# A third of gate/up's Strassen products moved out of the main loop, and up's multiplication moved from GpSimd to VectorE

## The chip, the cores and the metric

The kernel runs on one core of one Trainium2 chip. The metric is the device time of one execution in microseconds (us); of several runs the median counts. TensorE (PE) multiplies, VectorE (DVE) and ScalarE (ACT) work on SBUF and on PE's eight result banks, GpSimd (POOL) works on SBUF, and SyncE (SP) issues most DMAs.

## The reference

One decoder block on 2048 tokens of 1024 channels, in float32: a mixer (stick-breaking attention in 8 heads beside a causal pooling) and a dense SwiGLU layer, each between two RMS norms and modulated by a vector c. The change touches the second part alone:

```
h = rmsnorm(x, g_ffn_pre) * (1.0 + scale_f) + shift_f
f = (silu(h @ w_gate) * (h @ w_up)) @ w_down          # 1024 -> 2816 -> 1024
x = x + gate_f * rmsnorm(f, g_ffn_post)
```

## The kernel before

A float32 operand is split into a high and a low part, and a product of two blocks is three matmuls (`mm3`: high by high, low by high, high by low). The first half of the program computes the conditioning vectors, the mixer's projections, the attention and the mixer's output. From about 980 us on it works on gate, up and down. Everything below is about that half.

**Strassen's products.** `h @ w_gate`, `h @ w_up` and the multiplication by `w_down` are each done with seven products of half-size blocks in place of eight. For gate and up the blocks are halves of the 1024 channels (4 blocks of 128 each), the tokens in two halves of 512 within each half (`sb`) of the sequence, and the 2816 columns in 22 blocks of 128, taken as 11 pairs j and j + 11 (`HF` = 11). The weight blocks are a11, a12, a21, a22, with the sums s1 to s4; the token blocks are b11 to b22, with the sums t1 to t4 (L1557, `combine`). The seven products are p1 = a11·b11, p2 = a12·b21, s2·t2, s3·t3, s1·t1, a22·t4 and s4·b22. Each is 4 blocks x 3 = 12 matmuls of 128x512.

**The passes (`inner`, L1311).** p1 and p2 are done ahead of the main loop, in a pass of their own each (`q` = 0 and 1). A pass takes gate's and up's weights and both halves of the sequence as the four blocks of another Strassen scheme: per j seven products of 2 blocks x 3 = 6 matmuls (the banks a, e, f, b, h, i, d), 42 in place of 48. GpSimd makes the weight sums s12 and s34 (L1339 to L1347, four instructions of 256 words per j), ScalarE and VectorE split the operands (`split_by_bank`, L1169: a cast, a copy of it into a bank, a subtraction), VectorE combines the products, and the four results go to HBM (`keep`, L1366, tensor `pd`).

**Token operands.** A pass needs token sums of its own (`inner_sums`, L1196). Those of the second pass are made during the first (`second_operands`), and t1 to t4 for the main loop during the second (`main_operands`, L1618): GpSimd makes t3, t2, t1 and t4 from blocks loaded from `h2d` (the tiles `hs`), t4 is put away in HBM (`lated`) and fetched with b22 at the loop's start (`rest_operands`, L1651; tiles `b_raw` and `t_raw`). Beside that, GpSimd makes the sums of w_down's blocks for later (`down_sums`, L1564, tiles `wd`), one set of four at every 12th step from step 10 on.

**The main loop (`gate_up`, L1518; `matrix`, L1405).** For each half sb and each j it loads p1 and p2 (`px`), and does the five other products of gate and then of up, 12 matmuls each. VectorE takes each product from its bank: u2 = p1 + s2·t2 and so on, and the four results per matrix. Gate's result goes through Silu on ScalarE (L1524). Up's result is written to a tile `cu` in SBUF by VectorE (L1533), and GpSimd multiplies it into gate's (L1534). Then GpSimd makes four sums of the products (L1544) for down. Each half's loop is followed by down (seven products of 11 blocks).

**What sets the order.** The order on PE, ACT, DVE and POOL is that in which the program issues them, step after step (a step is one product, 6 or 12 matmuls); each engine takes its instructions in order and waits on semaphores. The step loop (L2059) issues, at step n: what was put `ahead` for n, the product's matmuls, what was due (`takes`), splits for up to six products ahead (`PAIRS`, L1986), and one piece of the side work (the token operands). SP's order is set by a scheduler. The second pass begins at step 77, the main loop at 154.

## Time and profile before

| | us |
|---|---|
| median of 3 runs | 2237.81 (2234.83 to 2240.35) |
| the profiled execution | 2236.15 |
| its span, first to last instruction | 2234.3 |
| first pass of gate/up, from its first matmul | 983.7 |
| main loop, first half, from | 1204.0 |
| down, first half, from | 1506.3 |
| main loop, second half, from | 1717.0 |
| down, second half, from | 2016.2 |

In the groups of instructions, `xN | busy, mean ns | idle before <-releaser` stands behind a line, an engine, an operation, the tile written and the tiles read: N instructions, their busy time in us, the mean of one in ns, the idle time of the engine ahead of them and what ended it. A row of waits reads: engine, what waited, for whom: us in total, times, longest. A row of stages gives the stretch in us, its length, busy time and number of instructions of PE, PEld (TensorE's weight load), DVE, ACT and POOL, then TensorE's granted clock, the DMA engines' busy share and GB/s. A row of the timeline gives start and duration, both in us.

### The profile page before, as it was taken

To read this page: it belongs to the slowest core of one execution; us is meant where nothing else is said; L and a number is where in the kernel's file an instruction comes from. 1 tells how busy PE (TensorE), PEld (TensorE's weight loads), DVE (VectorE), ACT (ScalarE), POOL (GpSimd) and SP (SyncE) were. 2 spreads that over 40 slices of the span, in tenths; PEclk is the share of its full clock that TensorE was granted. 3 is DMA by queue.
4 is the path that set the end of the run, shared out by engine and by line. 5 is a ranking of instruction groups with operands and counts; after the bars stand their busy time and mean duration, and the time that the engine had idled before them with its cause. 6 is when DMAs were issued, how large, how long until landed. Compare 5 with 4: busy or idle time off the path is not lost.

```text
span 2234.3 us, 34412 instructions
## 1 busy us (share of the span) xinstructions
PE 2201.7 (99%) x10481; PEld 1820.6 (81%) x10481; DVE 1604.3 (72%) x2386; ACT 1353.1 (61%) x2752; POOL 1300.4 (58%) x1702
## 2 busy tenths in 40 slices
PE   8999999999999999999999999999999999999998
PEld 6888888888888888878877888888888888888886
DVE  7874599999999965557767655566877656655566
ACT  6435599898989844457756555545555455544454
POOL 1452277787779955538875777762314887761003
PEclk9999999999999999999999999999999999999999
DMA  9986876534443456678999565558778755648664
GB/s 315 344 284 212 285 205 180 151 105 118 119 122 101 150 169 202 206 235 296 319 326 331 181 197 185 187 193 283 235 221 278 246 188 191 198 148 314 203 192 146
DMA packets 364213, 478.13 MB, mean 214 GB/s; under 512 B 23734, under 2 KB 211706, under 8 KB 361084
## 3 DMA queue, kind: packets, MB, share of 16 engines
q1 hardware_dynamic: 359836, 471.73, 65.8%
q10 hardware_dynamic: 4192, 4.20, 0.7%
q8 instruction: 83, 1.36, 0.3%
q14 instruction: 102, 0.84, 0.1%
HBM read 323.27 MB, written 152.57 MB: 213 GB/s over the span
## 4 chain that ended last, share of the span: by engine, by line
PE 54%; POOL 1%; DVE 1%; DMA 1%; issue 1%; ACT 1%; SPq 0%; DVEq 0%; ACTq 0%; POOLq 0%
PE t_u L69 4%; PE t_u L70 4%; PE t_u L71 4%; PE t_g L70 3%; PE t_g L69 3%; PE t_g L71 3%; PE dn0p L70 3%; PE dn0p L69 3%; PE dn0p L71 3%; PE dn1p L69 3%; PE dn1p L71 3%; PE dn1p L70 3%; PE mix L69 1%; PE mix L70 1%; PE mix L71 1%
## 5 line engine op out<-in xcount | busy, mean ns | idle before, releaser
L952 POOL TENSOR_TENSOR w<-sg,pr 128x512 f32<-128x512 f32 (+2 forms) x320 | 306.3, 957 | 46.4 <-DVE pr L947 14.5
L947 DVE TENSOR_TENSOR_SCAN pr<-pr,carry,begin 128x512 f32<-128x512 f32 x192 | 244.3, 1273 | 0.0
L931 ACT ACTIVATE sg<-z 128x512 f32<-128x512 f32 (+2 forms) x320 | 183.1, 572 | 50.8 <-PE z L929 40.5
L60 DVE TENSOR_TENSOR wtl<-wt,wth 128x512 fp32r<-128x512 f32 (+1 forms) x320 | 190.2, 594 | 19.0 <-ACT wth L59 16.8
L59 ACT CAST wth<-wt 128x512 fp32r<-128x512 f32 (+1 forms) x320 | 181.8, 568 | 11.7 <-PE wt L963 9.3
L933 ACT ACTIVATE pr<-z 128x512 f32<-128x512 f32 (+2 forms) x320 | 182.2, 569 | 0.0
L1534 POOL TENSOR_TENSOR s<-s,cu 128x512 f32<-128x512 f32 x88 | 115.9, 1318 | 111.6 <-DVE cu L1533 102.5
L963 PE MATMUL wt<-ident,w 128*128 128x128 f32 x1088 | 172.3, 273 | 1.5 <-POOL pr L943 1.1
L963 PEld LDWEIGHTS wt<-ident,w 128*128 128x128 f32 x1088 | 134.1, 140 | 32.7 <-POOL pr L943 1.8
L1524 ACT ACTIVATE s<-s 128x512 f32<-128x512 f32 x88 | 55.6, 633 | 163.1 <-DVE s L1523 161.6
L978 PE MATMUL av<-wth,vt 128*128 128x512 f32 (+1 forms) x320 | 126.2, 394 | 0.9 <-ACT o L983 0.8
L70 PE MATMUL dn0p<-w0p_l,g0p_h 128*128 128x512 f32 x308 | 119.9, 389 | 0.9 <-DVE w0p_l L60 0.9
L69 PE MATMUL dn0p<-w0p_h,g0p_h 128*128 128x512 f32 x308 | 119.8, 389 | 0.0
L71 PE MATMUL dn0p<-w0p_h,g0p_l 128*128 128x512 f32 x308 | 119.8, 389 | 0.0
L928 PE MATMUL z<-kt,qt 128*128 128x512 f32 (+2 forms) x320 | 118.6, 371 | 0.7 <-ACT pr L933 0.6
L979 PE MATMUL av<-wtl,vt 128*128 128x512 f32 (+1 forms) x320 | 117.7, 368 | 1.3 <-DVE wtl L60 1.2
L929 PE MATMUL z<-kt,qt 128*128 128x512 f32 (+2 forms) x320 | 116.9, 365 | 0.0
L69 PE MATMUL dn1p<-w1p_h,g1p_h 128*128 128x512 f32 x292 | 113.6, 389 | 0.0
L70 PE MATMUL dn1p<-w1p_l,g1p_h 128*128 128x512 f32 x292 | 113.6, 389 | 0.0
L71 PE MATMUL dn1p<-w1p_h,g1p_l 128*128 128x512 f32 x292 | 113.6, 389 | 0.0
L944 DVE TENSOR_TENSOR_SCAN pr<-pr,zero,begin 128x128 f32<-128x128 f32 (+3 forms) x128 | 111.5, 873 | 1.7 <-ACT pr L933 1.7
L1181 DVE TENSOR_TENSOR u_s_l<-u_s,rounded 128x512 fp32r<-128x512 f32 x63 | 43.3, 688 | 90.8 <-ACT rounded L1180 90.8
(774 smaller groups left out, 7172.5 us busy)
## 6 DMA issues: line engine op xcount, KB each, us to landing
pd<-p_c SPq DMA_DIRECT2D x88, 256.0 KB, 4.6
px<-pd SPq DMA_DIRECT2D x22, 1024.0 KB, 6.5
g<-in_w_gate_dram SPq DMA_DIRECT2D x42, 512.0 KB, 4.2
u<-in_w_up_dram SPq DMA_DIRECT2D x42, 512.0 KB, 5.3
wc<-in_w_cond_dram SPq DMA_DIRECT2D x32, 512.0 KB, 7.5
qt<-qd SPq DMA_DIRECT2D x64, 256.0 KB, 4.0
kt<-kd SPq DMA_DIRECT2D x96, 128.0 KB, 3.3
vt<-vd SPq DMA_DIRECT2D x48, 256.0 KB, 3.8
```

The lines of the kernel that those rows point to most:

```text
L59: nc.scalar.copy(hi, src)
L60: low.tensor_tensor(lo, src, raw(hi), ALU.subtract)
L69: nc.tensor.matmul(ps, lh, rh, start=first and i == 0, stop=False)
L70: nc.tensor.matmul(ps, lh, rl, start=False, stop=False)
L71: nc.tensor.matmul(ps, ll, rh, start=False, stop=last and i == n - 1)
L928: nc.tensor.matmul(z[:, 0:L], qt[:, 0, i * P:(i + 1) * P], keys, start=True, stop=False)
L931: nc.scalar.activation(sg[:, 0:L], z[:, 0:L], AF.Sigmoid, scale=0.125)
L933: nc.scalar.activation(pr[:, 0:L], z[:, 0:L], AF.Sigmoid, scale=-0.125)
L947: nc.vector.tensor_tensor_scan(keys, keys, begin, carry, ALU.mult, ALU.bypass)
L952: nc.gpsimd.tensor_tensor(w[:, 0:L], sg[:, 0:L], pr[:, 1:L + 1], ALU.mult)
L963: nc.tensor.transpose(wt[:, i * P:(i + 1) * P], wss[u][i][:, b * P:(b + 1) * P], ident)
L978: nc.tensor.matmul(av[:, lo0:], vb, wh[:, lo0:], start=first, stop=False)
```

## The change

A third product, a22·t4, leaves the main loop for a third pass (`NQ` = 3), so that the steps before the main loop are 231 and the loop has four products per matrix and j. The third pass's token operands (t4 of both halves of the sequence and their inner sums) are made on GpSimd during the second pass (`third_operands`), the main loop's t1 to t3 during the third (now three sums per block in place of four), and t4 no longer goes through HBM. The sets of sums for down stand at the steps of `DOWN_AT`: five in the first pass, three in the second and three in the third (before: six begin in the first pass and five in the second). In `inner_sums` the first difference goes from VectorE to GpSimd, but not for the first pass's operands.

In the main loop p1 and the third product are copied by ScalarE into a result bank (`to_bank`), so that VectorE's add reads the bank; up's add now writes its result back into the bank and VectorE multiplies it into gate's tile, in place of `cu` and GpSimd. px has six blocks in place of four (one load in the second half of the sequence, two in the first). Banks are given out anew: the main loop has five banks for products and three for the copies.

```
+NQ = 3
+DOWN_AT = (10, 22, 34, 46, 58, 82, 106, 130, 156, 176, 196)
-    pd = [dt(f"pd{sb}", [P, NF // 2, 4, TB]) for sb in range(2)]
+    pd = [dt(f"pd{sb}", [P, NF // 2, 2 * NQ, TB]) for sb in range(2)]
-    MAIN = ("t2", "t3", "t1", "t4", "b22")
+    MAIN = ("t2", "t3", "t1", "b22")
...
-        nc.vector.tensor_tensor(x11, x12, x11, ALU.subtract)
+        (nc.vector if by is split else nc.gpsimd).tensor_tensor(x11, x12, x11, ALU.subtract)
...
-                (nc.scalar if m in (2, 5) else nc.sync).dma_start(st[n].rearrange("p (k n) -> p k n", k=HK), rows_of(src, q * HK, j))
+                (nc.scalar if m in (4, 5) else nc.sync).dma_start(st[n].rearrange("p (k n) -> p k n", k=HK), rows_of(src, min(q, 1) * HK, j + q // 2 * HF))
...
+        banked = {}
+        def to_bank(q):
+            if low_ps is not None:
+                banked[q] = low_ps(f"p{q}{name}")
+                nc.scalar.copy(banked[q], first(q))
...
         def take_p6(ps):
-            st["u2"] = plus("u2", ps, next(first_two()))
+            st["u2"] = plus("u2", ps, first(0))
+            take(0, 0, banked.get(0), first(1), first(0))
         def take_p7(ps):
             st["u3"] = plus("u3", ps, st["u2"])
+            take(1, 0, banked.get(2), st["u3"], first(2))
...
-             step("a22", "t4", lambda ps: take(1, 0, ps, st["u3"]), 4 if turn_back else 1),
              step("s4", "b22", lambda ps: take(0, 1, ps, st["u4"]))]
...
             s = ss[i, tb]
-            u = ft("cu", f"cu{sb}_{j}_{i}{tb}")
-            nc.vector.tensor_tensor(u, ps, rest, ALU.add)
-            nc.gpsimd.tensor_tensor(s, s, u, ALU.mult)
+            if ps is None:
+                u = ft("cu", f"cu{sb}_{j}_{i}{tb}")
+                nc.vector.tensor_tensor(u, other, rest, ALU.add)
+                nc.gpsimd.tensor_tensor(s, s, u, ALU.mult)
+            else:
+                nc.vector.tensor_tensor(ps, ps, rest, ALU.add)
+                nc.vector.tensor_tensor(s, s, ps, ALU.mult)
...
+    def third_operands():
+        ys["p3"] = inner_tiles("p3", opools["0"], "ya", "v14", "v32", "y22")
...
+        for u in range(2 * HK):
+            t = 6 + 8 * u
+            for n, k in zip((3, 1, 0, 2), (6, 5, 4, 4)):
+                at(t - k if u else 0, lambda u=u, n=n: load(u, n))
+            for k, args in enumerate(((1, 3, 1, ALU.subtract), (0, 1, 0, ALU.add), (2, 2, 0, ALU.subtract))):
+                at(t + k, lambda u=u, args=args: add(u, *args))
+            if u % 2:
+                for k in range(8):
+                    at(t + 3 + k, lambda i=u // 2: more(i))
...
-    g_ps = banks(4, 2, 3, 0, 1, 5)
-    d_ps = banks(6, 7, 3, 0, 1, 5, 4, 2), banks(4, 2, 1, 5, 6, 7, 3, 0)
+    g_ps = banks(2, 3, 5, 4, 0)
+    d_ps = banks(6, 7, 1, 4, 0, 5, 3, 2), banks(0, 5, 3, 2, 6, 7, 1, 4)
```

What stands on GpSimd in the second pass, around the second block of tokens. `hs` are the token tiles and sums, `wd` the sums for down, `p_4` the weight sums of j = 4. Before:

```order
L1342 TENSOR_TENSOR p_4_s_14783<-p_4_s_14783,p_4_320_14683 128x256
L1561 TENSOR_TENSOR hs_1_1_14617<-hs_1_3_14677,hs_1_1_14617 128x512
L1346 TENSOR_TENSOR p_4_s_14798<-p_4_320_14683 128x256
L1347 TENSOR_TENSOR p_4_s_14798<-p_4_320_14683,p_4_s_14783 128x256
L1561 TENSOR_TENSOR hs_1_0_14649<-hs_1_1_14617,hs_1_0_14649 128x512
L1561 TENSOR_TENSOR wd_512_14751<-wd_512_14755,wd_512_14751 128x512
L1561 TENSOR_TENSOR hs_1_3_14677<-hs_1_3_14677,hs_1_0_14649 128x512
L1561 TENSOR_TENSOR wd_0_14749<-wd_512_14751,wd_0_14749 128x512
L1561 TENSOR_TENSOR wd_512_14755<-wd_512_14755,wd_0_14749 128x512
L1561 TENSOR_TENSOR hs_1_2_14721<-hs_1_2_14721,hs_1_0_14649 128x512
```

Now, where L1642 are the token sums and L1205 to L1209 the inner sums:

```order
L1205 TENSOR_TENSOR hs_0_2_14443<-hs_0_2_14604,hs_0_2_14443 128x256
L1206 TENSOR_TENSOR hs_0_2_14604<-hs_0_2_14604 128x256
L1342 TENSOR_TENSOR p_4_s_14763<-p_4_321_14652 128x256
L1343 TENSOR_TENSOR p_4_s_14763<-p_4_s_14763,p_4_321_14652 128x256
L1208 TENSOR_TENSOR hs_0_2_14604<-hs_0_2_14604,hs_0_2_14443 128x256
L1209 TENSOR_TENSOR hs_0_2_14443<-hs_0_2_14443,hs_0_2_14604 128x256
L1347 TENSOR_TENSOR p_4_s_14779<-p_4_321_14652 128x256
L1348 TENSOR_TENSOR p_4_s_14779<-p_4_321_14652,p_4_s_14763 128x256
L1642 TENSOR_TENSOR hs_1_1_14725<-hs_1_3_14710,hs_1_1_14725 128x512
L1642 TENSOR_TENSOR hs_1_0_14748<-hs_1_1_14725,hs_1_0_14748 128x512
L1642 TENSOR_TENSOR hs_1_2_14750<-hs_1_2_14750,hs_1_0_14748 128x512
```

Three token sums take the place of four for a unit, there are eight units in place of four, and the inner sums have come in between; of the sums for down a set stands in this stretch before, and none now.

What stands on VectorE while up's products of j = 8 are taken, in the first half of the sequence. `t_u` and `b_u` are products in their banks, `u2u` to `u4u` partial sums, `s` gate's results, `g_9_s_l` low parts of the next weights. Before:

```order
L1454 TENSOR_TENSOR u2u_8_18088<-t_u_8_18051,px_8_17705 128x512
L1533 TENSOR_TENSOR cu_8_00_18090<-px_8_17705 128x512
L1181 TENSOR_TENSOR g_9_s_l<-g_9_s_17998,rounded 128x512
L1454 TENSOR_TENSOR u3u_8_18114<-t_u_8_18075,u2u_8_18088 128x512
L1181 TENSOR_TENSOR g_9_s_l<-g_9_321_17887,rounded 128x512
L1533 TENSOR_TENSOR cu_8_11_18138<-t_u_8_18101,u3u_8_18114 128x512
L1454 TENSOR_TENSOR u4u_8_18141<-t_u_8_18101,u2u_8_18088 128x512
```

Now, where `p0u` and `p2u` are the copies in the bank:

```order
L1450 TENSOR_TENSOR u2u_8_19094<-t_u_8_19055,px_8_18698 128x512
L1547 TENSOR_TENSOR p0u_8_19051<-p0u_8_19051,px_8_18698 128x512
L1548 TENSOR_TENSOR s_8_00_18983<-s_8_00_18983,p0u_8_19051 128x512
L1182 TENSOR_TENSOR g_9_s_l<-g_9_321_18900,rounded 128x512
L1450 TENSOR_TENSOR u3u_8_19121<-t_u_8_19081,u2u_8_19094 128x512
L1547 TENSOR_TENSOR p2u_8_19077<-p2u_8_19077,u3u_8_19121 128x512
L1548 TENSOR_TENSOR s_8_10_19015<-s_8_10_19015,p2u_8_19077 128x512
L1182 TENSOR_TENSOR g_9_s_l<-g_9_s_19053,rounded 128x512
L1450 TENSOR_TENSOR u4u_8_19148<-t_u_8_19108,u2u_8_19094 128x512
```

Behind each of up's adds stands the product that GpSimd had, and it reads what the add has just written.

What stands on SP ahead of the main loop. `b_raw` and, in the change, the tiles `hs_*_3` are b22; `t_raw` is t4. Before:

```order
L1516 DMA px_0_15625<-pd_164 128x2048
L1367 DMA pd_165<-p_9_c_15685 128x512
L1659 DMA b_raw<-h2d_124 128x512
L1659 DMA b_raw<-h2d_125 128x512
L1659 DMA b_raw<-h2d_126 128x512
L1659 DMA b_raw<-h2d_127 128x512
L1659 DMA t_raw<-late_158 128x512
L1659 DMA t_raw<-late_159 128x512
```

Now (b22's other three blocks stand further up):

```order
L1627 DMA hs_2_3_17025<-h2d_126 128x512
L1368 DMA pd_161<-p_7_c_16753 128x512
L1368 DMA pd_160<-p_8_c_16797 128x512
L1368 DMA pd_161<-p_8_c_16811 128x512
L1368 DMA pd_160<-p_8_c_16826 128x512
L1420 DMA u_0_321_16850<-in_w_up_dram 128x8x128
L1368 DMA pd_161<-p_8_c_16860 128x512
L1420 DMA g_1_320_17002<-in_w_gate_dram 128x8x128
L1368 DMA pd_160<-p_9_c_16900 128x512
L1368 DMA pd_161<-p_9_c_16915 128x512
L1368 DMA pd_160<-p_9_c_16927 128x512
L1520 DMA px_0_16902<-pd_160 128x2048
```

b22's loads have moved ahead of px, and t4's are gone.

More of the change, by code (lines that the diff above doesn't have):

```diff
@@ L1378, in take_p5 @@
         def take_p5():
[L1379 removed]
+            st["u4"] = t = ft("gf" if not q and m and m % 2 == 0 else "u4", f"u4{name}")
             if not q:
@@ L1554, in gate_up @@
         g[0].ahead.insert(0, (8, lambda: first_products_load(sb, j)))
+        if not sb:
+            g[0].ahead.insert(1, (8 if j else 2, lambda: third_products_load(j)))
         return g[:3] + u[:3] + g[3:] + u[3:] if sb == at == 0 else g + u
@@ L1635, in main_operands @@
             done, coming = [], list(order) if i + 1 < HK else []
-            for at, (n, t) in enumerate(itertools.chain(combine(nc.gpsimd, *(raw[i, k] for k in range(4))), [(None, None)] * 2)):
+            sums = itertools.islice(combine(nc.gpsimd, raw[i, 0], raw[i, 1], None, raw[i, 3]), 3)
+            for at, (n, t) in enumerate(itertools.chain(sums, [(None, None)] * 2)):
                 if done:
                     put(*done.pop(), split_by_bank)
-                if n == "t4":
-                    later(2, lambda i=i, t=t: nc.sync.dma_start(lated[i], t))
-                elif n:
+                if n:
                     done.append((ops[n], cols, t))
@@ L1951, in back, with main @@
             nonlocal g_ps, low_ps
-            g_ps, low_ps = (banks(1, 5, 4, 2, 6), None) if first else (banks(7, 3, 0, 1, 5, 6), banks(4, 2))
+            g_ps, low_ps = (banks(0, 5, 3), None) if first else (banks(2, 6, 7, 1, 4), banks(0, 5, 3))
+        def main():
+            nonlocal low_ps
+            low_ps = banks(6, 7, 1)
         r, at, left = [], {}, []
-        for q in range(2):
-            at[second_operands if q == 0 else main_operands] = len(r)
+        for q in range(NQ):
+            at[(second_operands, third_operands, main_operands)[q]] = len(r)
             for j in range(HF):
@@ L1961, in halves @@
         at[rest_operands] = len(r) - 2
-        for i in range(HF):
+        for i, k in enumerate(DOWN_AT):
             for n, op in zip((0, 6, 7, 8, 9), down_sums(i)):
-                r[10 + 12 * i + n].ahead.append((0, op))
+                r[k + n].ahead.append((0, op))
         for sb in range(2):
@@ L1967, in halves @@
                 s = gate_up(sb, (n - 1) % HF if sb else n, n)
+                if not sb and not n:
+                    s[0].ahead.insert(0, (0, main))
                 if sb and n < 2:
-                    s[0].ahead.append((0 if n == 0 else 5, lambda n=n: back(n == 0)))
+                    s[0].ahead.insert(0, (0 if n == 0 else 5, lambda n=n: back(n == 0)))
                 r += s[:1] + left + s[1:]
```

120 lines of the change are left out of this document (61 added, 59 removed).

## The prediction

> **What bounds the kernel now.** The page's first part, busy time by engine, and then the stages of the second half with each engine's busy time, the granted clock, the DMA share and GB/s:
>
> ```profile
> PE 2201.7 (99%) x10481; PEld 1820.6 (81%) x10481; DVE 1604.3 (72%) x2386; ACT 1353.1 (61%) x2752; POOL 1300.4 (58%) x1702
> ```
> ```profile
> 1003.00:1102.00 99.00, 99.00 (x439) 81.99 (x438) 75.72 (x126) 72.11 (x138) 81.33 (x87) 1.00 0.90 301
> 1102.00:1204.00 102.00, 98.34 (x432) 80.36 (x430) 77.35 (x127) 62.75 (x117) 80.52 (x80) 1.00 0.98 329
> 1260.00:1500.00 240.00, 240.00 (x1061) 198.72 (x1060) 138.32 (x211) 122.47 (x210) 181.10 (x140) 1.00 0.59 190
> ```
> TensorE (PE) is busy in all of the first pass of gate/up (1003 to 1102) and of the main loop (1260 to 1500), at the full clock of 1.00. Only the second pass (1102 to 1204) loses time, 3.7 of 102 us, and there the DMA engines are at 0.98. A busy PE is no proof that it works at its peak, so I read the spacing of its instructions in the timeline: the first matmuls of two neighbouring products of the main loop, 12 matmuls apart, and of two products of the second pass, 6 apart.
>
> ```profile
> 1218.02 0.39 PE L69 MATMUL t_u<-t3h,u_s_h 128*128 128x512 f32 x1
> ...
> 1220.74 0.39 PE L69 MATMUL t_u<-t1h,u_s_h 128*128 128x512 f32 x1
> ```
> ```profile
> 1145.04 0.39 PE L69 MATMUL ep<-v14p2h,p_s_h 128*128 128x512 f32 x1
> ...
> 1146.40 0.39 PE L69 MATMUL fp<-v32p2h,p_s_h 128*128 128x512 f32 x1
> ```
> 2.72 / 12 and 1.36 / 6 are both 0.2267 us. So a matmul costs 0.2267 us of the span in either place; its duration of 0.39 us overlaps its neighbours'. The Trainium skill, "TensorE: Matmul & The Clock Gate", section Back-to-back issue gap, gives 131 ns sustained for 512 columns; by it the sum below would be 66 x 0.131 = 8.6 us. The trace does not agree; its 0.2267 is used.
>
> PE's waits, whole span, the rows that lie behind 980 us:
>
> ```profile
> PE f_pt L134 <- DVE p_s_l L1181: 2.5, 1, 2.5
> PE ap L69 <- DVE u2p L1385: 2.1, 1, 2.1
> PE t_u L69 <- DVE p_c L1371: 1.4, 1, 1.4
> PE ip L69 <- ACT p1p L1376: 1.0, 1, 1.0
> PE dn0p L70 <- DVE w0p_l L60: 0.9, 1, 0.9
> PE ep L69 <- ACT p1p L1376: 0.9, 1, 0.9
> PE ep L69 <- DVE p_c L1371: 0.7, 1, 0.7
> ```
> Two (2.5 and 1.0) lie at the entry to the first pass, which the change leaves nearly alone. Three (2.1, 0.9, 0.7) are the second pass's 3.7 us, 1.4 is the entry to the main loop, 0.9 lies in down's first half. What ends last in the second pass stands in the chain of waits of that stretch:
>
> ```profile
> 1170.02 1.25 POOL hs L1561
> 1171.27 1.24 POOL wd L1561
> 1172.50 1.24 POOL hs L1561
> 1173.77 0.63 ACT t2h L1173
> ```
> GpSimd (POOL) is late with the token sums (hs), ScalarE (ACT) waits for one of them, and what is queued behind it on ACT reaches PE late.
>
> **What leaves and comes on PE.** The third product (a22 by t4) leaves the main loop: 11 pairs of columns x 2 matrices x 2 halves of the tokens x 12 matmuls = 528, at 0.2267 us 119.7 us. It comes back as a third pass of 11 x 7 products x 6 = 462 matmuls, 104.7 us. Net 66 matmuls, **-15.0 us**. No reason excludes that this whole term counts, as PE is what ends last nearly everywhere; it is lost only where another engine becomes late. So each cover is worked out, stage by stage.
>
> **The third pass's own engines.** It does per pair of columns (42 matmuls, 9.52 us) what the second does now. In the second pass's row above DVE is busy 77 and ACT 63 of 102 us, with the preparation of token operands included. The third pass has less to prepare (12 sums of 512 words on POOL in place of 16). Both hide behind PE. Cost 0; without that cover it would be what goes over 9.52 us per pair.
>
> **POOL in the second pass.** This is the tight place. The groups of POOL in it, and POOL's waits there:
>
> ```profile
> L1561 POOL TENSOR_TENSOR wd<-wd,wd 128x512 f32<-128x512 f32 x20 | 25.9, 1296 | 10.7 <-DMA wd<-in_w_down_dram 7.4 <-DMA hs<-h2d 2.4 <-DMA pd<-p_c 0.6
> L1561 POOL TENSOR_TENSOR hs<-hs,hs 128x512 f32<-128x512 f32 x16 | 20.7, 1295 | 4.1 <-DMA hs<-h2d 4.0
> L1341 POOL TENSOR_TENSOR p_s<-p 128x256 f32<-128x256 f32 x9 | 6.7, 742 | 0.6 <-DMA p<-in_w_up_dram 0.6
> ```
> Afterwards the pass holds 24 token sums (8 units of 3) and 12 sums for down (three sets of four, at steps 82, 106 and 130; the row's 20 are five sets), each 1.30 us: 46.8 us. At 0.74 us each it holds 16 inner sums and 44 weight sums: 44.4 us. Together 91 of 104.7 us, where now it is 80.5 of 102 and over 10 more of waiting for DMAs. Between the first token sum (step 83) and the last inner sum (step 145) stand 36 long and 50 short ones in the order, 46.8 + 37.0 = 83.8 us, against 62 steps x 1.36 = 84.3 us of PE. That is 99%: POOL keeps up only if it hardly waits. Two things give it room. The last operand is written at step 148 and read at 156, 8 steps or 10.9 us later; and half as many sets for down leave fewer loads to wait for. The pass's DMAs move tiles of 256 KB, as the stored products do:
>
> ```profile
> pd<-p_c SPq DMA_DIRECT2D x88, 256.0 KB, 4.6
> ```
> 44 products stored are 11.5 MB, 22 loads of weights 5.8, down's sums 6.3 (12 read, 12 written), 32 loads of tokens 8.4, together 32.0 MB in 104.7 us or 306 GB/s, under the row's 329. I take the stalls of this pass at what they are now, 3.7 us, a change of **0**. From below, all 3.7 go. From above, POOL's waits stay at 14.8 us (10.7 + 4.1) on top of 83.8: 98.6 - 84.3 = 14.3 us late, of which nothing is covered: +14.3 - 3.7 = +10.6 us.
>
> **Moving the multiplication.** Of the 88 multiplications of up none stays on POOL. In a pair of columns (96 matmuls, 21.8 us, now 27.2) DVE has 8 low parts, 6 sums, 8 adds and 4 products: 26. The nearest rows for the new product (one operand in the bank, one in SBUF, result in SBUF) are the low part against `rounded`, then the add that it follows; the POOL row is what goes:
>
> ```profile
> L1181 DVE TENSOR_TENSOR u_s_l<-u_s,rounded 128x512 fp32r<-128x512 f32 x27 | 18.6, 689 | 38.9 <-ACT rounded L1180 38.9
> ...
> L1533 DVE TENSOR_TENSOR cu<-t_u,u3u 128x512 f32<-128x512 f32 x16 | 11.1, 692 | 13.4 <-PE t_u L71 12.5 <-POOL u_s L1439 0.9
> ```
> ```profile
> L1534 POOL TENSOR_TENSOR s<-s,cu 128x512 f32<-128x512 f32 x36 | 46.9, 1302 | 49.6 <-DVE cu L1533 49.6
> ```
> 26 x 0.69 = 17.9 of 21.8 us, 82%, where the main loop's row says 138 of 240 (58%). The up half alone has 15 of them in 10.9 us. Starts of DVE in the timeline, two independent instructions and then one that reads what the one before wrote:
>
> ```profile
> 1306.61 0.69 DVE L1454 TENSOR_TENSOR u2u<-t_u,px 128x512 f32<-128x512 f32 x1
> 1307.21 0.69 DVE L1533 TENSOR_TENSOR cu<-px 128x512 f32<-128x512 f32 x1
> 1307.81 0.68 DVE L1181 TENSOR_TENSOR g_s_l<-g_s,rounded 128x512 fp32r<-128x512 f32 x1
> ```
> ```profile
> 1065.75 0.69 DVE L1393 TENSOR_TENSOR u3p<-hp,u2p 128x512 f32<-128x512 f32 x1
> 1066.47 0.69 DVE L1371 TENSOR_TENSOR p_c<-ep,u3p 128x512 f32<-128x512 f32 x1
> ```
> Spacing 0.60, and 0.72 behind a dependence. The up half: 15 x 0.60 + some 8 x 0.12 = 10.0 of 10.9 us; gate's 11 take under 8. If it runs over, five product banks and operands split six products ahead hold PE for some 4 products (10.9 us) until gate's half catches up. The Trainium skill, "VectorE: DVE Perf Modes", section The DRAIN you can't avoid, lets no next operation start before the pipe is empty, which speaks against loading DVE more: 15 x 0.69 = 10.4 of 10.9 us. The 0.60 spacing does not bear that out. Cost **0**; bounds 0 and the end of the third rival below.
>
> POOL keeps eight sums of weights and four of the products, by the page's row
>
> ```profile
> L1544 POOL TENSOR_TENSOR gs<-s,s 128x512 f32<-128x512 f32 x44 | 60.8, 1381 | 3.4
> ```
> 8 x 1.30 + 4 x 1.38 = 15.9 of 21.8 us. That gains nothing, since PE doesn't wait for it in this loop.
>
> The new copies into the bank, 86, go to ACT; its rows in the main loop, and the nearest one to the copy (a full bank, in the second pass):
>
> ```profile
> L1524 ACT ACTIVATE s<-s 128x512 f32<-128x512 f32 x36 | 22.8, 632 | 68.4 <-DVE s L1523 67.0 <-DMA ga0s<-gs 1.4
> L1180 ACT COPY rounded<-u_s_h 128x512 f32<-128x512 f32 x36 | 21.3, 591 | 1.1
> ...
> L1173 ACT CAST u_s_h<-u_s 128x512 fp32r<-128x512 f32 x27 | 16.5, 610 | 14.8 <-PE b_u L70 10.3 <-POOL u_s L1446 4.5
> ```
> ```profile
> L1376 ACT COPY p1p<-ap 128x512 f32<-128x512 f32 x10 | 5.9, 587 | 21.0 <-PE ap L71 21.0
> ```
> Per pair 8 splits at 0.61 + 0.59 (cast, then the copy `rounded`), 4 Silu at 0.63 and 4 copies at 0.59: 14.5 of 21.8 us. A copy waits for its px load, and behind it on ACT are the splits for products six steps on; a late px would cost PE only beyond some 4 products. Cost 0.
>
> **Entry to the main loop.** Now the first px load, four of b22 and four of t4 go out nearly together; afterwards b22's stand ahead of px on the SP queue and t4's are gone, but px comes in two loads, each waiting for a tile of a pass that is ending. The nearest price is the 1.4 us wait there now. I keep it: **0**, from -1.4 to +1.4. The main loop's extra load is half as much px again, 0.5 MB per 21.8 us, 24 GB/s on a row of 190: 0.
>
> **Down and its ends.** Same work on other banks, 12 token sums for 16 in its first half; the 0.9 us may go. 0, from -0.9 to +0.9.
>
> **Sum.** The profiled execution took 2236.15 us (span 2234.3), 1.7 under the median of 2237.81, within the three runs' 2234.83 to 2240.35. 2236.15 - 15.0 = 2221.2; by the median **2222.8 us**.
>
> **Rivals.**
> *The waits go as well.* Fewer loads in the second pass and b22 ahead of px take away 3.7 + 1.4 + 0.9 = 6.0 us: 2216.8. For it: every one of these waits follows a DMA or POOL. Against: POOL has more to do there. 0.16.
> *POOL becomes the bound of the second pass.* Worked out above, from +3 to +10.6 us: 2226 to 2233.4. For it: 99%. Against: a POOL that lags finds its loads landed, and so waits less. 0.24.
> *Slower: the token loads close a circle.* A unit's last token tile takes the slot of the unit before, so it loads only once the third sum there has read it, and the next two sums wait for it: landing + 2 x 1.30 us per unit, against 8 steps or 10.9 us. SP is in order, so product stores, and through their tiles DVE, queue behind the waiting load. The landing of the token loads in the second pass:
>
> ```profile
> DMA to landing us min/median/max: 3.3/4.7/6.5
> ```
> Free up to 8.3 us. The gain is used up, and 6.7 us more, when 8 x (landing - 8.3) reaches 21.7, from a landing of 11.0 us. At 12 us: 29.6 - 15.0 = +14.6, or 2252.4. Against: 6.5 at most now, under a higher load. 0.07, with DVE in the main loop: were its 26 operations to take 0.85 us each (22.1 us), it would lose 0.3 x 22 pairs = 7 us, no more.
>
> **How the numbers follow.** Forecast 0.53, rivals 0.16, 0.24 and 0.07. About 0.3% (6.7 us, to 2231.1) is what a measurement of this kernel can tell. Faster: 0.53 + 0.16 and 0.08 of POOL's = 0.77; same: its other 0.16; slower 0.07. The range takes the lower rival and POOL's upper end: 2217 to 2234.
>
> **What would show it.** Right: 66 matmuls fewer at 0.2267; PE whole in the third pass and both main loops; PE's waits behind 980 us about 9.5 us. Wrong: waits on POOL's sums or on ACT behind them around steps 83 to 156 (POOL as the bound); SP waiting for the token sums with landings over 8 us (the circle); PE waiting in the main loop for a bank that DVE holds.

## The result, and the profile after

The changed kernel takes **2316.27 us** (median of 4 runs, 2314.20 to 2318.91), the kernel before 2238.85 (4 runs, 2234.83 to 2240.35). The ratio is 1.0349, with a 95% interval of 1.0331 to 1.0367: slower by 77 us, where 15 us less were forecast. The forecast of 2222.8 is missed by 93.5 us. (The title's "third" is to be read as one product, the third to leave the loop after p1 and p2: five products per matrix become four.)

The stages of the second half, from the starts of their first matmuls in the timelines. "Forecast" is the kernel before with the prediction's terms (104.7 us for the pass, 264 matmuls at 0.2267 us less per main loop, the rest unchanged):

| us | before | forecast | after |
|---|---|---|---|
| passes of gate/up | 220.2 | 324.9 | 320.5 |
| main loop, first half | 302.4 | 242.5 | 274.8 |
| down, first half | 210.7 | 210.7 | 215.2 |
| main loop, second half | 299.2 | 239.4 | 299.4 |
| down, second half, to the end | 218.1 | 218.1 | 220.7 |

The passes came out 4.4 us better than forecast. All of the loss lies in the two main loops (32.3 and 60.0 us) and in the steps of down behind them. The page's busy time by engine, and the windows of the second pass, the third pass and the two main loops (length, busy time of PE, PEld, DVE, ACT, POOL, granted clock, DMA share, GB/s):

```profile
PE 2228.1 (96%) x10415; PEld 1816.3 (78%) x10415; DVE 1690.6 (73%) x2555; ACT 1412.2 (61%) x2879; POOL 1242.9 (54%) x1694
```
```profile
1096.00:1200.00 104.00, 104.00 (x461) 86.11 (x460) 82.71 (x137) 68.61 (x131) 90.53 (x100) 1.00 0.95 317
1200.00:1305.00 105.00, 105.00 (x465) 86.95 (x464) 82.63 (x135) 67.01 (x125) 65.81 (x67) 1.00 0.84 281
1330.00:1570.00 240.00, 224.22 (x938) 173.19 (x937) 159.53 (x250) 131.49 (x232) 141.43 (x111) 1.00 0.70 221
1820.00:2080.00 260.00, 227.00 (x916) 176.78 (x915) 163.03 (x254) 131.17 (x229) 148.91 (x118) 0.95 0.63 208
```
In both passes PE works without a gap. In the main loops it does not, and no other engine is near its limit there: DVE, the busiest, is at 66% and 63%. The second loop has a lower granted clock as well. PE's waits behind 980 us, the eight largest:

```profile
PE t_g L71 <- DVE s L1533: 23.1, 17, 3.5
PE b_g L71 <- DVE s L1548: 14.7, 17, 1.4
PE b_u L71 <- DVE s L1533: 6.0, 18, 1.4
PE t_g L71 <- DVE u3u L1450: 4.2, 11, 0.4
PE dn1p L71 <- DVE s L1548: 3.6, 2, 2.5
PE b_g L71 <- ACT b22h L1174: 3.2, 1, 3.2
PE f_pt L135 <- DVE p_s_l L1182: 2.4, 1, 2.4
PE dn0p L71 <- DVE s L1548: 2.4, 2, 1.2
```
PE waits for banks that DVE has not emptied: by gate's sum (s, L1533) or by up's multiplication (s, L1548). Yet DVE is idle a third of the time. What it waits for shows where gate's half of a pair runs. ACT in one such half, from one Silu (L1534) to the last, then DVE in the same stretch:

```profile
1443.96 0.63 ACT L1534 ACTIVATE s<-s 128x512 f32<-128x512 f32 x1 [2.54 <-DVE s L1533]
1444.50 0.60 ACT L1174 CAST u_s_h<-u 128x512 fp32r<-128x512 f32 x1
1445.13 0.59 ACT L1181 COPY rounded<-u_s_h 128x512 f32<-128x512 f32 x1
1447.86 0.63 ACT L1534 ACTIVATE s<-s 128x512 f32<-128x512 f32 x1 [2.14 <-DVE s L1533]
...
1451.65 0.63 ACT L1534 ACTIVATE s<-s 128x512 f32<-128x512 f32 x1 [2.02 <-DVE s L1533]
...
1454.84 0.63 ACT L1534 ACTIVATE s<-s 128x512 f32<-128x512 f32 x1 [0.91 <-DVE s L1533]
```
```profile
1429.03 0.68 DVE L1533 TENSOR_TENSOR s<-b_g,u4g 128x512 f32<-128x512 f32 x1
...
1443.25 0.68 DVE L1533 TENSOR_TENSOR s<-p0g,px 128x512 f32<-128x512 f32 x1
1445.81 0.69 DVE L1182 TENSOR_TENSOR u_s_l<-u,rounded 128x512 fp32r<-128x512 f32 x1 [1.89 <-POOL s L1558]
1446.42 0.68 DVE L1450 TENSOR_TENSOR u3g<-t_g,u2g 128x512 f32<-128x512 f32 x1
1447.13 0.69 DVE L1533 TENSOR_TENSOR s<-p2g,u3g 128x512 f32<-128x512 f32 x1
1449.73 0.69 DVE L1182 TENSOR_TENSOR u_s_l<-u_s,rounded 128x512 fp32r<-128x512 f32 x1 [1.90 <-ACT rounded L1181]
...
1450.93 0.68 DVE L1533 TENSOR_TENSOR s<-t_g,u3g 128x512 f32<-128x512 f32 x1
...
1454.12 0.68 DVE L1533 TENSOR_TENSOR s<-b_g,u4g 128x512 f32<-128x512 f32 x1
```
Read the two together: Silu (1443.96), cast, `rounded` on ACT; at its end (1445.72) DVE's low part (1445.81), u3, s; at its end (1447.82) the next Silu (1447.86). Six operations, each standing behind the one before, on two engines that take their queues in order: a **closed circle** of 3.90 us for a product that takes PE 2.72. (The releaser POOL in the third DVE row was done at 1444.88; `rounded` ends there.) DVE's four sums of gate stand at 1443.25, 1447.13, 1450.93 and 1454.12: 10.87 us for three products, 8.16 on PE. From the last sum of one pair (1429.03) to the first of the next (1443.25) it is 14.22 us for five products, 13.60 on PE: up's half, in which DVE is nearly full, can't make it good. So DVE's cycle is 10.87 + 14.22 = 25.09 us a pair, and PE, through its five banks, is held to it:

```profile
1429.86 0.47 PE L71 MATMUL t_g<-t2h,g_s_h 128*128 128x512 f32 x1 [0.18 <-DVE s L1533]
...
1440.35 0.47 PE L71 MATMUL b_g<-b22h,g_s_h 128*128 128x512 f32 x1 [1.01 <-DVE s L1548]
...
1454.95 0.47 PE L71 MATMUL t_g<-t2h,g_s_h 128*128 128x512 f32 x1 [0.19 <-DVE s L1533]
```
1454.95 - 1429.86 = 25.09 us, and 8 x 2.72 would be 21.76. (Each wait costs PE some 0.25 us more than its row says: at the 1.01 us of 1440.35 two matmuls start 1.40 and 0.31 us behind the ones before them, 1.26 over twice 0.2267.)

In the second loop something is added. 21.6 of t_g's 23.1 us behind gate's sum lie there, and ACT's waits in that loop (1795 to 2095 us) have a row that the first loop's have not:

```profile
ACT g_s_h L1174 <- POOL g_s L1442: 18.9, 8, 3.2
```
GpSimd's sum of gate's next weights comes late, and ScalarE's split waits for it inside the circle. In the run "circle closed" at the end of the experiments (SyncE's order pinned and a slot of its own at the turn, the circle as it is) this wait is gone, and the second loop takes 281.9 us in place of 299.4; which of the two edits did it is not shown.

The circle was there before. ACT in the kernel before, two Silus of neighbouring products:

```profile
1325.03 0.63 ACT L1524 ACTIVATE s<-s 128x512 f32<-128x512 f32 x1 [1.77 <-DVE s L1523]
...
1328.15 0.63 ACT L1524 ACTIVATE s<-s 128x512 f32<-128x512 f32 x1 [1.35 <-DVE s L1523]
```
3.12 us there too, more than PE's 2.72. But one in five products (s3·t3) had no Silu, the sum s11 stood ahead of u4, and DVE had room in up's half.

### The profile page after: what moved, and what is told of

The parts are those of the page before. It is cut to its first block, busy times and chain, and to the rows that moved or that the text cites. A ratio compares the mean times of both kernels' runs of the same rounds, so it can differ in the third digit from the quotient of the medians.

```text
span 2315.3 us, 34805 instructions
## 1 busy us (share of the span) xinstructions
PE 2228.1 (96%) x10415; PEld 1816.3 (78%) x10415; DVE 1690.6 (73%) x2555; ACT 1412.2 (61%) x2879; POOL 1242.9 (54%) x1694
## 5 line engine op out<-in xcount | busy, mean ns | idle before, releaser
L1534 ACT ACTIVATE s<-s 128x512 f32<-128x512 f32 x88 | 55.6, 632 | 163.1 <-DVE s L1533 160.6
L1182 DVE TENSOR_TENSOR g_s_l<-g_s,rounded 128x512 fp32r<-128x512 f32 x63 | 43.2, 685 | 95.0 <-ACT rounded L1181 93.1
L1558 POOL TENSOR_TENSOR gs<-s,s 128x512 f32<-128x512 f32 x44 | 58.4, 1326 | 100.4 <-DVE s L1548 78.0
```

## The experiments

**Theories.** 1: the circle. 2: the three banks that splits and copies share are held by the multiplications. 3: VectorE has too much to do with the multiplication itself. All edits are against the changed kernel unless said otherwise.

| run | median us | ratio to before, 95% interval |
|---|---|---|
| late Silu | 2239.39 | 1.0009, 1.0000 to 1.0018 |
| s11 ahead of u4 | 2310.63 | 1.0331, 1.0315 to 1.0346 |
| multiplication on GpSimd | 2270.03 | 1.0147, 1.0132 to 1.0162 |
| no copies into banks | 2309.34 | 1.0323, 1.0306 to 1.0340 |
| three passes, old operations | 2284.72 | 1.0217, 1.0203 to 1.0231 |
| low part late | 2253.83 | 1.0077, 1.0063 to 1.0090 |
| late Silu, own slot | 2233.36 | 0.9983, 0.9974 to 0.9992 |
| before, multiplication on VectorE | 2236.81 | 0.9997, 0.9988 to 1.0006 |
| late Silu, own slot, two on GpSimd | 2253.33 | 1.0071, 1.0058 to 1.0084 |
| late Silu, own slot, all on GpSimd | 2263.06 | 1.0116, 1.0100 to 1.0131 |
| longer Silu | 2355.36 | 1.0527, 1.0513 to 1.0542 |
| longer Silu, late, own slot | 2247.49 | 1.0045, 1.0031 to 1.0059 |
| no multiplication | 2242.41 | 1.0024, 1.0014 to 1.0033 |
| late Silu, own slot, no multiplication | 2302.85 | 1.0287, 1.0269 to 1.0304 |
| pinned SyncE: circle closed | 2304.34 | 1.0303, 1.0285 to 1.0322 |
| pinned SyncE: circle open | 2250.54 | 1.0069, 1.0051 to 1.0087 |
| pinned SyncE: open, no multiplication | 2229.96 | 0.9970, 0.9960 to 0.9980 |
| pinned SyncE: open, all on GpSimd | 2261.43 | 1.0115, 1.0099 to 1.0131 |

**Late Silu.**

```
-            nc.scalar.activation(s, s, AF.Silu)
+            later(1, lambda: nc.scalar.activation(s, s, AF.Silu))
```


> The changed kernel with each Silu of the main loop issued one product later on ScalarE, so that it no longer stands between VectorE's sum and the next split. Theory 1 (a closed circle of in-order queues in gate's half: Silu, cast, rounded on ScalarE, then low part, u and sum on VectorE, then the next Silu; some 3.8 us per product where TensorE needs 2.72): the circle is open, most of the 80 us goes, 2225 to 2245 us, and TensorE's waits in the main loops fall from about 60 to under 20 us. Theory 2 (the three banks shared by the splits and the copies are held by the multiplications) and theory 3 (VectorE is overloaded by the multiplication itself): neither banks nor VectorE's work change, 2305 to 2318 us.

2239.39 us: 77 us less, as theory 1 had it. The first main loop falls from 274.8 to 244.3 us. The longest wait that stays stands at the turn into the second loop (257.0 us). PE, ACT and POOL of this run there:

```profile
1814.98 0.77 PE L71 MATMUL t_g<-t2h,g_s_h 128*128 128x512 f32 x1 [8.32 <-DVE s L1533]
```
```profile
1812.21 0.62 ACT L1174 CAST g_s_h<-g_s 128x512 fp32r<-128x512 f32 x1 [11.05 <-POOL g_s L1442]
```
```profile
1807.26 1.26 POOL L1558 TENSOR_TENSOR gs<-s,gs 128x512 f32<-128x512 f32 x1 [8.16 <-DMA ga1s<-gs]
```
POOL's fourth sum waits for a store to free its slot, the weight sums stand behind it on POOL, the split behind them on ACT, the product behind that.

**s11 ahead of u4.** The two lines of `take_p5` change places. In up's half u4 then reads the bank after the sum was written back, so s01 has another value; the operations are the same.

> The changed kernel with the old order in take_p5: the sum s11 ahead of u4 on VectorE. Theory 1: one VectorE operation of 0.6 to 0.7 us leaves the circle in one of four products of gate, 22 times: 13 to 15 us less, 2300 to 2304 us. Theories 2 and 3: the same operations and banks, within 4 us of 2316.

2310.63 us, 5.6 us less, under half of what one operation in 22 circles should give. The sign fits theory 1, the size doesn't, and why was not settled.

**Multiplication on GpSimd.**

```
-                nc.vector.tensor_tensor(ps, ps, rest, ALU.add)
-                nc.vector.tensor_tensor(s, s, ps, ALU.mult)
+                here = sb and j == HF - 1
+                u = ps if here else ft("cu", f"cu{sb}_{j}_{i}{tb}")
+                nc.vector.tensor_tensor(u, ps, rest, ALU.add)
+                (nc.vector if here else nc.gpsimd).tensor_tensor(s, s, u, ALU.mult)
```


> The changed kernel with up's multiplication back on GpSimd through an SBUF tile in 21 of the 22 pairs of columns (the pair at which the halves turn keeps it on VectorE); copies into the banks and the order of u4 stay. Theory 3: VectorE has 4 operations fewer per pair, the loss goes, 2225 to 2250 us. Theory 1: gate's half is as before, only up's share of the waits (b_u 6.0, a part of b_g's 14.7 us) can go, 2285 to 2318 us. Theory 2: the banks are free one operation (0.6 us) sooner in up's half, 2290 to 2310 us.

2270.03 us, 46 us less: between the ranges, and in none of the three. Theory 1 alone is too small, theory 3 alone too large. VectorE's share in up's half counts, as what could have made good the circle's delay.

**No copies into banks.**

```
-            if low_ps is not None:
+            if turn_back and low_ps is not None:
...
-                nc.gpsimd.tensor_tensor(s, s, u, ALU.mult)
+                nc.vector.tensor_tensor(s, s, u, ALU.mult)
```


> The changed kernel without the copies of stored products into banks in 21 of the 22 pairs: both products are read from SBUF, and the sum for up goes to an SBUF tile and is multiplied there, on VectorE as well. The three banks then serve the splits alone, and ScalarE has 4 operations fewer per pair. Theory 2: no split waits for a bank that a multiplication holds (43 us of ScalarE's waits in the two loops), most of the loss goes, 2235 to 2260 us. Theory 1: the circle keeps its six operations and loses at most the copies that stand in ScalarE's queue in gate's half, 2 x 0.59 us per pair, 26 us: 2290 to 2316 us. Theory 3: VectorE's work is the same, 2305 to 2318 us.

2309.34 us, 7 us less; theory 2's 2235 to 2260 is far off. It is no clean test, since operations of VectorE that now read SBUF alone got longer: the sum cu<-px took 1.39 us on the mean in 218 us of the first loop (the next run shows how).

**Three passes, old operations.** The last three edits together, with `take(1, 1, ...)` ahead of u4; at the one pair that keeps the write into the bank, up's u4 again reads the sum.

> The changed kernel with its three passes and four products, but with the operations around them as they were: multiplication on GpSimd through SBUF, stored products read from SBUF without copies, s11 ahead of u4 (at the pair where the halves turn up keeps VectorE and its copies). Theory 1, the circle alone: gate's half still has four products in a row that each go through Silu, split, u and sum, so loss remains; from the run with the multiplication on GpSimd (2270.0) the two other edits take 6 + 7 us by their own runs: 2250 to 2262 us. Theory 3 (the new work on VectorE and ScalarE is the loss): all of it goes, and the prediction's sum holds, 2218 to 2234 us. GpSimd stands at 21.1 of 21.8 us per pair, which can add to either.

2284.72 us, over both ranges. The new operations are not what made the change slow: with the old ones it is slow as well, and 15 us slower than with the copies kept and the multiplication on GpSimd. What the trace has to set against those 15 us are DVE's rows: first two groups in 218 us of the first loop (from SBUF alone, and with one operand in a bank), then two operations and, last, POOL's two beside the second of them:

```profile
L1533 DVE TENSOR_TENSOR s<-px 128x512 f32<-128x512 f32 x9 | 16.0, 1782 | 0.0
...
L1450 DVE TENSOR_TENSOR u3g<-t_g,u2g 128x512 f32<-128x512 f32 x9 | 6.1, 682 | 0.0
```
```profile
1403.44 0.68 DVE L1544 TENSOR_TENSOR cu<-px 128x512 f32<-128x512 f32 x1
...
1410.99 1.79 DVE L1533 TENSOR_TENSOR s<-px 128x512 f32<-128x512 f32 x1
```
```profile
1410.94 1.28 POOL L1446 TENSOR_TENSOR u_s<-u,u_s 128x512 f32<-128x512 f32 x1
1412.19 1.74 POOL L1550 TENSOR_TENSOR s<-s,cu 128x512 f32<-128x512 f32 x1
```
A sum of two SBUF operands takes DVE 0.68 us in a gap of POOL and 1.79 beside it, inside the circle; with an operand in a bank it is 0.68 on the mean, with POOL busy 192 of the 218 us. The changed kernel's copies into banks avoid that: its sums of p0g and p2g take 0.68 and 0.69. That these longer sums make up the 15 us is argued, not shown: no run takes them away alone.

**Low part late.**

```
+        low = lambda: nc.vector.tensor_tensor(lo, src, both, ALU.subtract)
+        later(2, low) if late else low()
```
(`late` for gate's operands in the main loop; it comes behind the next product's u and sum.)

> The changed kernel with Silu where it was, but with VectorE's low part of gate's operands issued behind the next product's u and sum instead of ahead of them. It opens the circle on the other engine, with the same instructions on ScalarE in the same order. Theory 1: the same gain as with the late Silu, 2235 to 2255 us. Rival: what helped there was Silu's place in ScalarE's queue by itself (splits that are no longer late for TensorE): no gain, 2305 to 2320 us.

2253.83 us, 62 us less, with Silu where it was. The circle opened on the other engine gives most of it as well, with ScalarE's instructions and their order unchanged.

**Late Silu, own slot.**

```
-            s3, s2, s4 = (ft("gs", f"g{n}{sb}_{j}") for n in ("s3", "s2", "s4"))
+            s3, s2, s4 = (ft("p1" if sb and at == 0 and n == "s4" else "gs", f"g{n}{sb}_{j}") for n in ("s3", "s2", "s4"))
```


> Late Silu, and at the turn of the halves the last of GpSimd's four sums (s4) goes to an SBUF slot of its own (p1, idle there) instead of a gs slot that waits for a store. In the run with the late Silu alone GpSimd waited 8.2 us there, ScalarE 11.1 us behind it and TensorE 8.3 us behind that, at 1806 to 1815 us, with a granted clock of 0.84 in that stretch. If the slot is the cause: 9 to 13 us less than 2239.4, 2226 to 2231 us. If the loads of weights behind it in SyncE's queue are late anyway: 2234 to 2240 us.

2233.36 us, 6 us less where 9 to 13 were expected of the slot: the 8.3 us wait is gone, but the second loop still takes 252.2 us. This version beats both kernels, the one before by 0.17% only: less than the prediction's 0.3%, though the interval of these 11 runs leaves out 1.

**Before, with the multiplication on VectorE.** One word in the kernel before, `nc.gpsimd` to `nc.vector` at L1534.

> The kernel before with up's multiplication on VectorE (both operands in SBUF), nothing else changed: four operations more per pair of columns in a loop of five products per matrix, 27.2 us. Theory 1: five products leave VectorE and the circle slack, within 5 us of before. Theory 3: VectorE's multiplication delays what is queued behind it whatever the loop, at least a third of the 46 us that its return to GpSimd gave: slower by 15 us or more.

2236.81 us, no change, although the operation took longer than the 0.69 us that it takes with an operand in a bank (a stretch of the first loop):

```profile
L1534 DVE TENSOR_TENSOR s<-s,cu 128x512 f32<-128x512 f32 x37 | 33.8, 914 | 1.3
```
In a loop of five products VectorE has room for it.

**Two, or all, on GpSimd with the circle open.** The edit of the third run, for `tb` = 1 alone (and gate's s11 ahead of u4), or for all.

> Late Silu and the own slot at the turn, and two of up's four multiplications (s11 and s01) back on GpSimd through SBUF, with s11 ahead of u4 in gate's half only. In the run it is built on, TensorE still waited 7.4 us in 14 places for a bank that an up multiplication on VectorE holds (b_g behind L1548), and lost about half a microsecond per pair. If VectorE's up half (15 operations in 10.9 us) is what is left: those waits go, 2224 to 2230 us. If GpSimd, now at 18.5 of 21.8 us per pair, delays sums of weights instead: 2231 to 2240 us.

> Late Silu and the own slot at the turn, with all of up's multiplications back on GpSimd (21 pairs of 22). With the circle closed that return gave 46 us. If VectorE's multiplications cost time only because they leave the up half no room to make good what the circle lost in gate's half: with the circle open it gives next to nothing, 2226 to 2240 us. If they cost by themselves (theory 3): 15 us or more less than 2233.4, under 2219 us.

2253.33 and 2263.06 us: slower than with VectorE, against both expectations. ACT waits longer for POOL's weight sums (50 and 47 us for g_s in 218 us of the first loop; 26 in the run with the own slot, which has the multiplication on VectorE).

**A longer Silu, inside and outside the circle.**

```
             nc.scalar.activation(s, s, AF.Silu)
+            nc.scalar.copy(s, s)
```


> The changed kernel with one more full copy on ScalarE (some 0.6 us) behind each Silu, on the same tile, so inside the circle; 88 of them. Theory 1: each adds its time to a product of gate: 88 x 0.6 = 53 us, 2355 to 2372 us. Theories 2 and 3: ScalarE has 14.5 of 21.8 us per pair, 2.4 more are hidden and neither banks nor VectorE have more to do: 2312 to 2325 us.

> The same additional copy behind each Silu, but with the Silu issued one product later and the own slot at the turn: the same work on ScalarE, outside the circle. Theory 1: it hides, within 6 us of 2233.4, 2228 to 2240 us. If ScalarE's load as such were what costs: again some 50 us more than without it, 2270 to 2290 us.

2355.36 us inside, 39 us more, 0.44 us for each of 88 copies; outside 2247.49, 14 us more. ACT's load is the same. Theory 1 holds in kind, its 53 us were too many, and the work outside is not quite free.

**No multiplication.** The line of L1548 left out, so that the output lacks this product, with Silu early and then late.

> The changed kernel with up's multiplications in the bank left out, all but two at the turn of the halves (the sum for up stays, the product with the Silu is missing from the output), so that VectorE has them not and GpSimd doesn't either. In the changed kernel's steady state a pair takes 25.09 us: 10.87 us from the first to the last of gate's four sums on VectorE (the circle, three products) and 14.22 us from there to the next first one (up's half, VectorE full). If these two add up: four operations at about 0.66 leave the second, 10.87 + 11.6 = 22.5 us per pair, 2.6 x 22 = 57 us less, 2245 to 2265 us. If the circle alone is the loss: 2300 us or more. If the multiplication alone is (theory 3): all goes, 2218 to 2230 us.

> Late Silu and the own slot at the turn, with the same multiplications left out. If VectorE's multiplication costs nothing of note once the circle is open: the 7.4 us that TensorE waited for its banks go at most, 2225 to 2234 us. If it is a cost of its own: 15 us or more less than 2233.4, under 2219 us. What stays above 2222.8 in this run is neither circle nor multiplication.

2242.41 us with the circle closed, 74 us less and just under the sum's range: behind the loop's entry all products of the first loop stand 2.72 us apart. So an up half with room makes good all that gate's half loses; the sum 10.87 + 11.6 = 22.5 us a pair was too large, as PE's own 21.76 is reached. With the circle open, 2302.85: 69 us more than the own-slot run, for less work. SyncE and POOL of that run, one pair in the later half of the first loop:

```profile
1427.34 0.38 SPq L1420 DMA_DIRECT2D g<-in_w_gate_dram  x1
...
1440.97 0.38 SPq L1420 DMA_DIRECT2D g<-in_w_gate_dram  x1
...
1442.08 0.39 SPq L1420 DMA_DIRECT2D u<-in_w_up_dram  x1
...
1454.82 0.39 SPq L1420 DMA_DIRECT2D g<-in_w_gate_dram  x1
```
```profile
1435.86 1.29 POOL L1435 TENSOR_TENSOR g_s<-g,g 128x512 f32<-128x512 f32 x1 [4.28 <-DMA g<-in_w_gate_dram]
...
1439.68 1.27 POOL L1446 TENSOR_TENSOR g_s<-g,g_s 128x512 f32<-128x512 f32 x1
...
1448.54 1.28 POOL L1435 TENSOR_TENSOR u_s<-u,u 128x512 f32<-128x512 f32 x1 [7.59 <-DVE t_u L1547]
...
1452.39 1.30 POOL L1446 TENSOR_TENSOR u_s<-u,u_s 128x512 f32<-128x512 f32 x1
```
A second circle, of 27.48 us (1427.34 to 1454.82): gate's load, its landing, four sums, then the load that waits for the last of them, up's load behind it on SyncE, its landing, four sums, and gate's load again. (The releaser DVE in the third POOL row happened to end there; in the pairs around it the row names u's load.) In the run with the multiplication up's load is issued ahead of gate's wait and the sums follow one another. The order on SyncE is chosen by a scheduler at each build, and differs between most of these kernels.

**Pinned SyncE.** So the last four share one order, that in which the code issues (`ET.SP` joins the manual schedule), and the own slot.

> The changed kernel with the own slot at the turn and with SyncE's DMA issues pinned to the order in which the code writes them, as those of the other engines are (in the runs so far SyncE's order was chosen anew at each build and came out differently: stores and weight loads change places between edits). The circle is closed. Theory 1: the loss doesn't hang on SyncE's order, 2290 to 2318 us. Rival (the new order of SyncE, not the circle, made the changed kernel slow and the late Silu only shuffled it): 2225 to 2260 us.

> The same pinned order of SyncE, with each Silu one product later. Theory 1: the circle's loss goes, 55 to 80 us less than the run with it closed, 2225 to 2245 us. Rival (order of SyncE): no difference to that run beyond 10 us.

> The same pinned order, late Silu, and up's multiplications in the bank left out (the output lacks the product with the Silu). The earlier run of this kind took 2302.9 us with 27.5 us per pair: in SyncE's chosen order the weight loads stood behind waits for GpSimd, in a circle of load, sums and next load. If that order was the cause, that goes, and VectorE's multiplication with the circle open is priced cleanly: within 10 us under the run with it if it costs little, 2220 to 2240 us; 15 us or more under it if it is a cost of its own. If leaving it out is slow for another reason: 2280 us or more again.

> The same pinned order, late Silu, and all of up's multiplications but those of the turn on GpSimd. If the 30 us that this cost in the earlier run (2263.1 against 2233.4) came with SyncE's chosen order: 2222 to 2242 us. If they are GpSimd's own load, 21.1 of 21.8 us per pair: 2250 to 2270 us.

Closed 2304.34, open 2250.54, open without the multiplication 2229.96, open with all of it on GpSimd 2261.43: SyncE's order is not what made the change slow, though the gain of 53.8 us is just under theory 1's 55 to 80 and 2250.54 lies over its range. The first main loop's window of closed, open, and open without the multiplication, the first two with the largest row of PE's waits in the loops:

```profile
1330.00:1540.00 210.00, 195.64 (x821) 151.18 (x821) 139.83 (x220) 115.00 (x203) 124.02 (x97) 1.00 0.64 216
```
```profile
PE b_g L71 <- DVE s L1548: 18.6, 19, 1.3
```
```profile
1330.00:1540.00 210.00, 209.23 (x920) 172.07 (x919) 158.15 (x250) 128.34 (x228) 141.05 (x111) 1.00 0.73 246
```
```profile
PE b_g L71 <- DVE s L1548: 5.5, 13, 1.7
```
```profile
1330.00:1540.00 210.00, 210.00 (x928) 173.91 (x927) 142.20 (x220) 138.93 (x239) 144.30 (x114) 1.00 0.79 264
```
The circle is worth 53.8 us here and, with the circle open, the multiplication 20.6: in this order of SyncE a cost of its own. In the scheduler's order the own-slot run, with the multiplication, lies only 3.4 us above the run without it here, so the 20.6 hold for the pinned order. (Leaving it out also frees banks sooner, so in these 20.6 theories 2 and 3 are not told apart.) Only 2.7 of the 20.6 fall in the first loop (246.5 to 243.8 us); the rest is in down's stages (6.0 and 3.7) and the second loop (8.4), which begin behind what VectorE has left over; PE's rows have 4.4 us of waits for up's multiplications at the second down (dn1p), the rest of this reading is argued. GpSimd is no way out: 10.9 us over VectorE, as was expected if its own load is what costs.

## Why the prediction was wrong

- **66 matmuls at 0.2267 us: right.** The page counts 10481 - 10415 = 66, and the run without circle and multiplication has its first loop at 243.8 us, forecast 242.5.
- **The passes, and GpSimd in the second one: right, a little too dear.** GpSimd was busy 90.5 of 104 us and PE lost nothing. The 3.7 us went, the lower bound. Both rivals on GpSimd and the token loads fell.
- **Moving the multiplication, cost 0: the step that failed.** It said that five banks and operands split ahead hold PE for some four products "until gate's half catches up", because "gate's 11 take under 8" us. That was a sum of busy times. Gate's 11 operations stand in a circle with ACT's and take 10.87 us for three products where PE needs 8.16, so a pair takes DVE 25.09 us where PE needs 21.76, and the five banks only pass the delay on. The trace of before had it: 3.12 us from Silu to Silu. The row of Silu's waits that the prediction quoted (67.0 us on DVE) and DVE's row of waits on `rounded` (38.9) are the two halves of the circle, and the prediction drew nothing from them. With the up half full there is no room to catch up; the run without the multiplication has that room, and there gate's half does catch up.
- **Copies on ACT, cost 0 because 14.5 of 21.8 us are busy: not refuted, not shown.** Again a busy time; a copy that was added behind each Silu, inside the circle, cost 0.44 us each.
- **Entry to the main loop, 0 to 1.4 us either way: too narrow.** PE's wait there, for b22, is 3.2 us where it was 1.4. The turn of the halves was not looked at, and cost 6 us once the circle was open (the run with the own slot).
- **Down, 0.9 us either way: +4.5 and +2.6.** PE's rows there have 2.4 and 3.6 us of waits for up's last multiplications on VectorE (dn0p, dn1p).
- **VectorE's operations at 0.85 us in the third rival: no,** 0.68 to 0.69 in the banks.

The 93.5 us, along the pinned runs: own slot and pinned order 11.9 (2316.3 to 2304.3, not told apart; the second loop alone is 17.5 us shorter, down behind the first loop 4.9 longer), the circle 53.8, the multiplication 20.6, and 7.2 that stay between 2230.0 and the forecast, mostly in the second loop (248.5 for 239.4). Of the cause of those 7.2 nothing was tried. The split holds for this order of taking things away. Taken first, from the changed kernel, the late Silu is worth 76.9 us and the multiplication 73.9 (2242.4, circle closed): the loss needs both, a circle longer than PE's time and an up half without room, and to remove either takes away nearly all of the slow-down against the kernel before.

## What to carry to other kernels

A sum of busy time per engine says that an engine can keep up only if nothing it does depends on another engine's next answer. Where two in-order engines wait for each other, add up one trip around (operation after operation, from two neighbouring starts in the timeline) and set it against the time of the bounding engine: a trip that is longer is already lost, and only hidden where products without it, or a half with room, follow. And before two builds are compared, see whether the queue that a scheduler orders is the same in both: it was worth 17 us here with the circle open (2233.4 and 2250.5) and in the run without the multiplication a poor order hid what leaving it out was worth.

## What the runs showed of the hardware

**A short wait can cost more than itself.** PE of the changed kernel in the second main loop, after a wait of 3.51 us:

```profile
1850.06 0.47 PE L71 MATMUL t_g<-t2h,g_s_h 128*128 128x512 f32 x1 [3.51 <-DVE s L1533]
...
1851.33 0.63 PE L72 MATMUL t_g<-t2l,g_s_h 128*128 128x512 f32 x1
1851.75 0.63 PE L73 MATMUL t_g<-t2h,g_s_l 128*128 128x512 f32 x1
```
The matmuls come 0.43 us apart in place of 0.2267, for some 3.4 us, and the granted clock is halved; the row of 3 us in this stretch has it at 0.51:

```profile
1851.20:1854.20 3.00, 3.00 (x8) 0.51 1.03 306
```
In this loop seven such stretches, some 60 matmuls, cost 11.5 us on top of the waits. Each follows a wait of 2.1 to 3.5 us, and none a wait of 1.8 us or less; but not every wait of that length brings one (2.99 us at 2067.22 did not). The second loop, with waits of that length at the start of gate's half, took 24.6 us longer than the first, where PE's repeated waits are 1 us or less; the stretches are 11.5 of it. The Trainium skill, "TensorE: Matmul & The Clock Gate", section What's actually happening, has the clock halved after an idle window of about 3.4 us and back after a busy one; the length of most stretches agrees (one lasts 5.5 us), but waits of 2.1 us brought them on here.

**VectorE and GpSimd in SBUF.** 128x512 in float32, in the run with three passes and the old operations. Two SBUF operands: 0.68 us alone, 1.79 beside GpSimd; one operand in a bank: 0.68 on the mean with GpSimd as busy. The Trainium skill, "GPSIMD Engine Reference", section Specifications, names this contention for VectorE's instructions with two SBUF inputs; the rows above agree and give it a size.
